# The low halves of every second K and V weight tile by accumulating DMA, and S5 chunks issued one place earlier

## The chip, the cores and the metric

The kernel runs on one core of one Trainium2 chip. The metric is the device time of one execution in microseconds (us). The engines are TensorE (PE, matmuls, with PEld for its weight loads), VectorE (DVE), ScalarE (ACT), GpSimd (POOL) and SyncE (SP, which here only issues DMAs). Everything is float32 in the reference; the kernel reaches that precision by splitting each operand into a high part of type float32r and a low part, which is the remainder.

## The reference

One encoder layer over 256 tokens of width 2048, then a final RMSNorm:

```python
hn = rms_norm(h, norm_mix_g); proj = hn @ w_in           # (256 x 2048) @ (2048 x 3072): conv a, conv gate, ssm u
yc = conformer_conv_group(conv_a, conv_gate, ...)        # a * sigmoid(gate), causal depthwise conv of width 31, layer norm, silu
ys = s5_group(ssm_u, ...)                                # complex diagonal scan over time, 64 groups, then gelu and a 1024 x 1024 GLU
h = h + concat(rms_norm(yc), rms_norm(ys)) @ w_out
hn = rms_norm(h, norm_mem_g); mem_n = rms_norm(mem, mem_norm_g)
h = h + mem_cross_attention(hn, mem_n, w_q, w_kv, w_o)   # kv = mem_n @ w_kv is (256 x 2048) @ (2048 x 4096)
h = h + peer(rms_norm(h), ...)                           # product-key experts, gathered rows of two 16384 x 2048 tables
return rms_norm(h, final_norm_g)
```

The change concerns `mem_n @ w_kv` (its first 2048 columns are K, the others V) and the order in which the parts of `s5_group` are issued.

## The kernel before

A planner orders the instructions of each engine: it takes the program in order, with priorities, and simulates the engines with its own costs; `tc.high_priority(offset=n)` lets what stands inside be ordered as if it had come n instructions earlier. On the chip each engine then runs its own list strictly in that order and waits on semaphores. Tile pools are rings: a tile with `bufs=n` can be written again when all readers of the tile n places before it are done.

`linear` (L147) is the matrix product of all large weights. For each chunk of 512 output columns it walks over eight pairs of 128 rows (index `j`, KG = 2). For each pair it

- loads a weight tile `w_raw` of 128 x 2 x 512 float32 (512 KB) by a DMA from SP (L155, a ring of five);
- on ACT casts it to `w_hi` (L162, a ring of three), on DVE subtracts to get `w_lo` (L163, a ring of three);
- on PE makes three products, activations high by weight high, high by low and low by high (L172 to L174 where the output has tokens on the partitions, as V has; L181 to L183 where it has columns on the partitions, as K and `w_in` have).

All of that but the matmuls is given AHEAD = 500 places of priority. Where a caller gives `whole`, the last pair (`j` = 7) is not split: `whole_matmuls` (L133) multiplies `w_raw` itself in full float32 (L143 for K and `w_in`, L140 for V), and its `w_raw` stays occupied until those matmuls are done. So a chunk of K or V has seven split tiles and one whole one; K and V have four chunks each, 56 split tiles and 8 whole ones.

The order of the program around the change is: the third part of `w_in` (ssm u), the set-up of S5 (tables, BT, CT), then `w_in` in four chunks a0, g0, a1, g1 (each the product of 512 columns; a is the conv input, g its gate), the norm of `mem`, four chunks of K, four of V, the GLU (`zh`, `zl`, weight `ssm_glu_w`), the norm of the S5 half, half of `w_out`, the convolution (L565 and L568: 248 DVE instructions of 128x256, last in the program and so with the lowest priority, but possible from the time that the gates are done), its norm, and the other half of `w_out`.

S5 works in eight chunks q. `s5_next` (L473) issues `s5_tables(q + 1)` (sines and cosines by ACT and DVE) and `s5_body(q)`: 24 small PE matmuls (L445), products and eight scans on DVE (L446 to L462), 32 PE matmuls (L466) and the update of `uT` on DVE (L469). It is issued with 700 places of priority. Before the change it is called after each of a0, g0, a1, g1 and after each K chunk: eight calls for eight chunks.

POOL has no work between its set-up and the end of this part of the kernel; it is used for gathers from 855 us on.

Of the kernel before, what the change touches and what calls it, by code (L numbers as in the profile page):

```python
# [9 lines left out]
F32 = mybir.dt.float32  # L10
F32R = mybir.dt.float32r
# [3 lines left out]
AF = mybir.ActivationFunctionType  # L15
ALU = mybir.AluOpType
# [4 lines left out]
P = 128  # L21
T = 256
NTT = T // P
D = 2048
KT = D // P
# [4 lines left out]
KG = 2  # L30
AHEAD = 500
# [29 lines left out]
W_IN, W_K, W_V = True, True, True  # L61
# [3 lines left out]
SETTLE_RATE = 2.4  # L65
SETTLE_AT = 185
LAG = 2
R_BY = ('AAAA', 'AAVA')


@with_exitstack
def trunk(ctx, tc, a, out, dbg=None):
    nc = tc.nc
    V, S, G, PE, SY = nc.vector, nc.scalar, nc.gpsimd, nc.tensor, nc.sync
# [45 lines left out]
    uctx = ctx.enter_context(ExitStack())  # L120
    with ExitStack() as wctx:
        atx = wctx.enter_context(ExitStack())
        wp = wctx.enter_context(tc.tile_pool(name="wp", bufs=3, side="right"))
        at = atx.enter_context(tc.tile_pool(name="at", bufs=1))
        psm = wctx.enter_context(tc.tile_pool(name="psm", bufs=3, space=PSUM))
        pst = wctx.enter_context(tc.tile_pool(name="pst", bufs=2, space=PSUM))
# [7 lines left out]
        def whole_matmuls(ps, x, raw, j, begin, end, rows_out):  # L134
            for i in range(KG):
                k = (j - (KT // KG - NWHOLE)) * KG + i
                first, last = begin and i == 0, end and i == KG - 1
                if rows_out:
                    for tt in range(NTT):
                        PE.matmul(ps[tt], x[:, k, tt * P:(tt + 1) * P], raw[:, i, :], start=first, stop=last)  # L140
                else:
                    for cb in range(4):
                        PE.matmul(ps[cb // 2][:, cb % 2, :], raw[:, i, cb * P:(cb + 1) * P], x[:, k, :],  # L143
                                  start=first and cb % 2 == 0, stop=last and cb % 2 == 1, skip_group_check=True)

        def linear(x, w, c0, ncol, evac, rows_out, kt=KT, korder=None, ahead=AHEAD, whole=None, cols=None):
            xh, xl = x  # L147
            js = korder or range(kt // KG)
            for n, (c, w_) in enumerate(cols or [(c, 512) for c in range(c0, c0 + ncol, 512)]):
                ncb = w_ // P  # L150
                ps = [psm.tile([P, 512] if rows_out else [P, 2, T], F32, name="mm", tag="mm") for _ in range(2)]
                for m, j in enumerate(js):
                    with tc.high_priority(offset=ahead):
                        raw = wp.tile([P, KG, w_], F32, name="w_raw", bufs=5)
                        SY.dma_start(raw, w[j * KG * P:(j + 1) * KG * P, c:c + w_].rearrange("(k p) c -> p k c", p=P))  # L155
                        full = whole is not None and j >= kt // KG - NWHOLE
                        if full:
                            whole_matmuls(ps, whole, raw, j, m == 0, m == len(js) - 1, rows_out)
                            continue
                        hi = wp.tile([P, KG, w_], F32R, name="w_hi")  # L160
                        lo = wp.tile([P, KG, w_], F32R, name="w_lo")
                        S.copy(hi, raw)  # L162
                        V.tensor_sub(lo, raw, hi.bitcast(F32))  # L163
                    for i in range(KG):
                        k = j * KG + i
                        first, last = m == 0 and i == 0, m == len(js) - 1 and i == KG - 1
                        ah, al = xh[k // 4][:, k % 4, :], xl[k // 4][:, k % 4, :]
                        if rows_out:
                            for tt in range(NTT):
                                o = ps[tt]  # L170
                                ts = slice(tt * P, (tt + 1) * P)
                                PE.matmul(o, ah[:, ts], hi[:, i, :], start=first, stop=False)  # L172
                                PE.matmul(o, ah[:, ts], lo[:, i, :], start=False, stop=False)  # L173
                                PE.matmul(o, al[:, ts], hi[:, i, :], start=False, stop=last)  # L174
                        else:
                            for cb in range(ncb):
                                o = ps[cb // 2][:, cb % 2, :]
                                end = cb % 2 == 1 or cb == ncb - 1
                                wh = hi[:, i, cb * P:(cb + 1) * P]
                                wl = lo[:, i, cb * P:(cb + 1) * P]  # L180
                                PE.matmul(o, wh, ah, start=first and cb % 2 == 0, stop=False, skip_group_check=True)  # L181
                                PE.matmul(o, wh, al, start=False, stop=False, skip_group_check=True)  # L182
                                PE.matmul(o, wl, ah, start=False, stop=last and end, skip_group_check=True)  # L183
                for half in range((ncb + 1) // 2):
                    evac(n, half, ps[half])
                yield n
# [9 lines left out]
        with ExitStack() as mctx:  # L196
# [276 lines left out]
            def s5_next():  # L473
                q = s5["q"]
                if q < CQ:
                  with tc.high_priority(offset=S5_AHEAD):
                    now = s5["tables"]
                    s5["tables"] = s5_tables(q + 1) if q + 1 < CQ else None
                    s5_body(q, now)
                    s5["q"] = q + 1  # L480

            for n in range(2):
                run(linear(xT, a["w_in"], n * 512, 512, ev_a(n), False, whole=xW if W_IN else None))
                s5_next()
                run(linear(xT, a["w_in"], CH + n * 512, 512, ev_g(n), False, whole=xW if W_IN else None))
                s5_next()
            memT, memW = load_mem(a["mem"], a["mem_norm_g"])
# [8 lines left out]
                S.copy(t, ps)  # L496
                SY.dma_start(v_dram[:, tt, 512 * n:512 * n + 512], t)

            for _ in linear(memT, a["w_kv_mem"], 0, D, ev_k, False, whole=memW if W_K else None):
                s5_next()  # L500
            kv_v = linear(memT, a["w_kv_mem"], D, D, ev_v, True, whole=memW if W_V else None)
            run(kv_v)
            for j in range(2):
                z = uT[:, 4 * j:4 * j + 4, :]
# [56 lines left out]
            for k in range(CW):  # L561
                for q in range(CQ):
                    src = cpad[:, q, k:k + T]
# [10 lines left out]
            for q in range(CQ):  # L574
                S.activation(acc[:, q, :], acc[:, q, :], AF.Silu, bias=colv[:, 2, q:q + 1],
                             scale=colv[:, 1, q:q + 1])
# [162 lines left out]
        for n in range((KD + 3) // 4):  # L739
            w = min(KD - 4 * n, 4)  # L740
# [256 lines left out]
    def settle():  # L997
        groups = P // 4
        for tt in range(NTT):
            held = {}  # L1000
            for n in range(groups + LAG):
                if n < groups:
                    held[n] = extract(routes[tt], n)
                    yield
                if n >= LAG:
                    pick(routes[tt], n - LAG, *held[n - LAG])
                    yield
                if tt and n < groups:
                    build(routes[0], n, R_BY[0], "ut", 2)
                    yield  # L1010
# [32 lines left out]
    for g in range(P // 4):  # L1043
        build(routes[1], g, R_BY[1], ("sy", "ut")[g % 2], 2)
    uctx.close()
# [68 lines left out]
    for tt, st in enumerate(sts):  # L1114
        for c, cs_ in enumerate([slice(DC, D)] + COLS):
            src = h3[tt][:, cs_] if c else accg[tt]
# [36 lines left out]
```

## Time and profile before

| | |
|---|---|
| median of 3 runs | 2125.04 us (2120.92 to 2128.39) |
| the profiled execution | 2121.98 us, span 2120.0 us |
| mean granted TensorE clock in it | 0.972 |
| busy shares of the span | PE 93%, DVE 83%, ACT 48%, POOL 35% |
| DMA issues of the weights concerned | `w_raw<-in_w_kv_mem` x64, 512.0 KB each |

In the views of the profile, a row of windows gives the busy time of each engine in a stretch of the span, the granted clock of TensorE as a part of 1, the share of the 16 DMA engines' time in use, and GB/s. A row of waits says who waited for whom, the us in total, how often, and the longest. A row of groups gives the engine, the operation, out<-in, the shape, the count, then busy us and mean ns of one, then the idle time just before. A row of the timeline gives start and length in us, and in brackets the idle time before and what ended it.

### The profile page before, as it was taken

How to read it: one execution, taken by the hardware profiler on the slowest of the kernel's cores; microseconds unless marked ns; L12 is line 12 of the kernel's file. 1: busy time of each engine (PE TensorE's matmuls, PEld its weight loads, DVE VectorE, ACT ScalarE, POOL GpSimd, SP SyncE). 2: the span in 40 equal slices, each digit the busy share in tenths (PEclk: the TensorE clock that was granted, in tenths of full speed). 3: DMA queues.
4: the chain of work that ended last, by engine and by line, in shares of the span. 5: the costliest groups of instructions: out<-in, count | busy, mean ns of one | idle time of the engine just before them, and what ended most of it. 6: DMA issues, size and time to landing. Idle time of an engine off the chain costs nothing.

```text
span 2120.0 us, 32032 instructions
## 1 busy us (share of the span) xinstructions
PE 1970.8 (93%) x11619; PEld 1698.4 (80%) x11619; DVE 1760.7 (83%) x2855; ACT 1024.5 (48%) x1746; POOL 736.2 (35%) x548
## 2 busy tenths in 40 slices
PE   8998798999999999899999999689879999999997
PEld 7987786668799988788888888577667888888886
DVE  5789999987665566999986667998888999899997
ACT  5764544436454454333333333578793444444444
POOL 0000000000000002535446665543218877677772
PEclk9999989999999999999999999899999999999998
DMA  7554454554865476798999999998629999999995
GB/s 246 166 179 154 125 149 130 161 177 139 291 222 193 140 232 221 283 321 319 317 336 402 402 406 391 370 327 275 205 90 318 373 348 337 348 336 340 336 340 187
DMA packets 199390, 563.41 MB, mean 266 GB/s; under 512 B 32050, under 2 KB 40866, under 8 KB 199105
## 3 DMA queue, kind: packets, MB, share of 16 engines
q1 hardware_dynamic: 141888, 318.08, 45.5%
q0 software_dynamic: 57344, 243.30, 30.5%
q8 instruction: 91, 1.49, 0.3%
q14 instruction: 67, 0.54, 0.1%
HBM read 549.38 MB, written 11.93 MB: 265 GB/s over the span
## 4 chain that ended last, share of the span: by engine, by line
PE 48%; DVE 25%; issue 13%; POOL 6%; DMA 5%; ACT 2%; SPq 0%; DVEq 0%; POOLq 0%; ACTq 0%
PE acc L1100 8%; PE acc L1101 8%; PE acc L1099 8%; DVE u L861 6%; POOL u L859 5%; PE mm L183 4%; PE mm L181 4%; PE mm L182 4%; DVE acc L568 3%; DVE w_lo L163 3%; PE mm L174 2%; PE mm L173 2%; PE mm L172 2%; PE y L932 1%; DMA hnT<-ib_dram 1%
## 5 line engine op out<-in xcount | busy, mean ns | idle before, releaser
L861 DVE SCALAR_TENSOR_TENSOR u<-u,hnF 128x1280 f32<-128x1280 f32 x256 | 388.6, 1520 | 86.0 <-DMA u<-in_peer_u,uidx 84.6
L1064 POOL DMA_INDIRECT v<-in_peer_v,vidx x256 | 385.7, 1507 | 178.5 <-DVE accg L1066 68.5
L859 POOL DMA_INDIRECT u<-in_peer_u,uidx x256 | 308.1, 1204 | 328.2 <-DVE u L861 254.0
L162 ACT CAST w_hi<-w_raw 128x1024 fp32r<-128x1024 f32 (+2 forms) x228 | 231.4, 1018 | 289.1 <-PE mm L182 125.7
L901 PE MATMUL sy<-hnT,ut 128*128 128x256 f32 x1536 | 357.0, 385 | 7.9 <-ACT ut L897 7.3
L163 DVE TENSOR_TENSOR w_lo<-w_raw,w_hi 128x1024 fp32r<-128x1024 f32 (+2 forms) x228 | 270.8, 1190 | 111.5 <-ACT w_hi L162 111.3
L901 PEld LDWEIGHTS sy<-hnT,ut 128*128 128x128 f32 x1536 | 287.3, 193 | 48.6 <-ACT ut L897 11.9
L103 ACT CAST vh<-vr 128x1472 fp32r<-128x1472 f32 x128 | 183.2, 1431 | 271.0 <-PE acc L1100 165.8
L1100 PE MATMUL acc<-vh,wl 128*128 128x512 f32 (+1 forms) x768 | 296.7, 386 | 4.4 <-DVE wl L1090 4.3
L183 PE MATMUL mm<-aT_hi,w_lo 128*128 128x256 f32 x960 | 273.2, 293 | 27.2 <-DVE w_lo L163 27.1
L1101 PE MATMUL acc<-vl,wh 128*128 128x512 f32 (+1 forms) x768 | 295.9, 386 | 0.0
L742 POOL TENSOR_TENSOR hnT<-aT_hi,aT_lo 128x1024 f32<-128x1024 f32 (+1 forms) x2 | 3.8, 1908 | 814.5 <-ACT w_hi L162 814.5
L181 PE MATMUL mm<-aT_hi,w_hi 128*128 128x256 f32 x960 | 279.0, 294 | 4.0 <-DVE sg L264 2.3
L1099 PE MATMUL acc<-vh,wh 128*128 128x512 f32 (+1 forms) x768 | 276.5, 385 | 3.2 <-ACT vh L103 2.2
L182 PE MATMUL mm<-aT_lo,w_hi 128*128 128x256 f32 x960 | 276.4, 290 | 0.0
L104 DVE TENSOR_TENSOR vl<-vr,vh 128x1472 fp32r<-128x1472 f32 x128 | 216.5, 1692 | 39.6 <-ACT vh L103 36.9
L1066 DVE SCALAR_TENSOR_TENSOR accg<-v,coef,accg 128x576 f32<-128x576 f32 x256 | 208.7, 815 | 12.0 <-DMA v<-in_peer_v,vidx 7.4
L183 PEld LDWEIGHTS mm<-aT_hi,w_lo 128*128 128x128 f32 x960 | 185.5, 197 | 34.9 <-DVE w_lo L163 31.5
L181 PEld LDWEIGHTS mm<-aT_hi,w_hi 128*128 128x128 f32 x960 | 188.5, 197 | 8.3 <-DVE sg L264 2.9
L182 PEld LDWEIGHTS mm<-aT_lo,w_hi 128*128 128x128 f32 x960 | 189.0, 197 | 1.3 <-issue 0.4
L897 ACT COPY ut<-ut 128x768 f32<-128x768 f32 x128 | 100.4, 801 | 165.8 <-PE ut L895 145.9
L1100 PEld LDWEIGHTS acc<-vh,wl 128*128 128x128 f32 x768 | 145.2, 189 | 35.8 <-DVE wl L1090 5.4
(345 smaller groups left out, 3368.6 us busy)
## 6 DMA issues: line engine op xcount, KB each, us to landing
vr<-in_peer_v SPq DMA_DIRECT2D x128, 736.0 KB
raw<-in_peer_u SPq DMA_DIRECT2D x128, 384.0 KB
w_raw<-in_w_kv_mem SPq DMA_DIRECT2D x64, 512.0 KB
w_raw<-in_w_in SPq DMA_DIRECT2D x48, 512.0 KB
w_raw<-in_w_out SPq DMA_DIRECT2D x32, 512.0 KB
w_raw<-in_w_q_mem SPq DMA_DIRECT2D x32, 512.0 KB
w_raw<-in_w_o_mem SPq DMA_DIRECT2D x32, 512.0 KB
hnT<-ib_dram SPq DMA_DIRECT2D x18, 256.0 KB
```

The source lines that it names most:

```text
L162: S.copy(hi, raw)
L163: V.tensor_sub(lo, raw, hi.bitcast(F32))
L181: PE.matmul(o, wh, ah, start=first and cb % 2 == 0, stop=False, skip_group_check=True)
L182: PE.matmul(o, wh, al, start=False, stop=False, skip_group_check=True)
L183: PE.matmul(o, wl, ah, start=False, stop=last and end, skip_group_check=True)
L859: G.indirect_dma_start(out=u, out_offset=None, in_=a["peer_u"].rearrange("e (q c) -> (e q) c", c=GU), in_offset=bass.IndirectOffsetOnAxis( ...
L861: V.scalar_tensor_tensor(u, u, 1.0, hnF[:, self.tt, :], op0=ALU.mult, op1=ALU.mult, accum_out=self.act[:, j:j + 1])
L901: PE.matmul(ps[:, b % 2, :], ut[:, k, :], hnT[:, k, :], start=k == 0 and b % 2 == 0, stop=k == KD - 1 and b % 2 == 1, skip_group_check=True)
L1064: G.indirect_dma_start(out=v, out_offset=None, in_=table, in_offset=bass.IndirectOffsetOnAxis(ap=vidx[tt][:, j:j + 1], axis=0))
L1099: PE.matmul(o, wh[:, tt, :], vh[:, cs_], start=b == 0, stop=False)
L1100: PE.matmul(o, wl[:, tt, :], vh[:, cs_], start=False, stop=False)
L1101: PE.matmul(o, wh[:, tt, :], vl[:, cs_], start=False, stop=b == NB - 1)
```

## The change

Three things change.

1. In the K and V products, tiles with odd place `m` in their chunk (1, 3 and 5; place 7 is the whole tile) get their low part in another way: ACT writes the negated, rounded tile into `w_lo`, and a DMA issued from POOL adds the weights to it from memory, reading the same 512 KB a second time. The DVE subtraction of these tiles is gone.
2. The rings are resized for every `linear`: `w_raw` five to four, `w_lo` three to four, `w_hi` stays three.
3. `s5_next()` is called once more ahead of a0, so each S5 chunk is issued one call earlier and the last call (after the fourth K chunk) finds nothing left to do.

```diff
+RAW_BUFS = 4
+HI_BUFS = 3
+LO_BUFS = 4
...
-        wp = wctx.enter_context(tc.tile_pool(name="wp", bufs=3, side="right"))
+        wp = wctx.enter_context(tc.tile_pool(name="wp", bufs=HI_BUFS, side="right"))
...
-                        raw = wp.tile([P, KG, w_], F32, name="w_raw", bufs=5)
-                        SY.dma_start(raw, w[j * KG * P:(j + 1) * KG * P, c:c + w_].rearrange("(k p) c -> p k c", p=P))
+                        raw = wp.tile([P, KG, w_], F32, name="w_raw", bufs=RAW_BUFS)
+                        src = w[j * KG * P:(j + 1) * KG * P, c:c + w_].rearrange("(k p) c -> p k c", p=P)
+                        SY.dma_start(raw, src)
...
                         hi = wp.tile([P, KG, w_], F32R, name="w_hi")
-                        lo = wp.tile([P, KG, w_], F32R, name="w_lo")
+                        lo = wp.tile([P, KG, w_], F32R, name="w_lo", bufs=LO_BUFS)
                         S.copy(hi, raw)
-                        V.tensor_sub(lo, raw, hi.bitcast(F32))
+                        if dma_lo and m % 2:
+                            S.activation(lo, raw, AF.Copy, scale=-1.0)
+                            G.dma_start(lo, src, accum_op=ALU.add)
+                        else:
+                            V.tensor_sub(lo, raw, hi.bitcast(F32))
...
+            s5_next()
             for n in range(2):
                 run(linear(xT, a["w_in"], n * 512, 512, ev_a(n), False, whole=xW if W_IN else None))
                 s5_next()
...
-            for _ in linear(memT, a["w_kv_mem"], 0, D, ev_k, False, whole=memW if W_K else None):
+            for _ in linear(memT, a["w_kv_mem"], 0, D, ev_k, False, dma_lo=True, whole=memW if W_K else None):
                 s5_next()
-            kv_v = linear(memT, a["w_kv_mem"], D, D, ev_v, True, whole=memW if W_V else None)
+            kv_v = linear(memT, a["w_kv_mem"], D, D, ev_v, True, dma_lo=True, whole=memW if W_V else None)
```

More of the change, by code (lines that the diff above doesn't have):

```diff
@@ L144, in whole_matmuls, with linear @@
                                   start=first and cb % 2 == 0, stop=last and cb % 2 == 1, skip_group_check=True)
-        def linear(x, w, c0, ncol, evac, rows_out, kt=KT, korder=None, ahead=AHEAD, whole=None, cols=None):
+        def linear(x, w, c0, ncol, evac, rows_out, kt=KT, korder=None, dma_lo=False, ahead=AHEAD, whole=None, cols=None):
             xh, xl = x
```

## The prediction

> **What bounds the kernel now.** I read the windows by stage first, then the waits inside the stage that the change touches, then its groups by shape, then single timelines. The change acts from about 100 us to about 500 us; before and behind that only the ring sizes differ.
>
> ```profile
> 100.00:120.00 20.00, 18.96 (x155) 17.73 (x154) 18.41 (x27) 10.43 (x13) 0.00 (x0) 0.95 0.60 177
> 120.00:140.00 20.00, 20.00 (x159) 16.88 (x159) 12.61 (x18) 11.13 (x25) 0.00 (x0) 0.96 0.58 185
> 160.00:460.00 300.00, 264.07 (x1668) 216.18 (x1667) 300.00 (x486) 132.86 (x179) 0.00 (x0) 0.94 0.49 148
> 460.00:500.00 40.00, 35.66 (x258) 31.51 (x257) 25.70 (x29) 21.06 (x23) 0.00 (x0) 0.96 0.48 154
> 560.00:580.00 20.00, 20.00 (x92) 15.98 (x91) 12.46 (x15) 8.75 (x14) 0.00 (x0) 1.00 0.99 307
> 600.00:700.00 100.00, 100.00 (x841) 100.00 (x840) 59.71 (x85) 49.32 (x70) 0.00 (x0) 1.00 0.53 175
> ```
>
> The columns are the stretch, its length, busy us of PE, PEld, DVE, ACT and POOL, the granted clock, the DMA share and GB/s. From 160 to 460 us DVE is busy for all 300 us: in this stretch DVE sets the pace, and in the others shown it has idle time. PE is second. Its 264.07 us at a clock of 0.94 are 264.07 x 0.94 = 248 us of work at full clock, so 300 us could at best become 248: 36 us are idle and 16 us are lost to the clock. From 600 us on PE is busy without a break.
>
> ```profile
> PE mm L183 <- DVE w_lo L163: 21.4, 9, 5.4
> PE mm L173 <- DVE w_lo L163: 10.3, 3, 5.5
> PE mm L181 <- DVE sg L264: 2.3, 1, 2.3
> ```
>
> ```profile
> ACT w_hi L162 <- PE mm L182: 60.7, 20, 12.0
> ACT w_hi L162 <- PE mm L174: 47.6, 19, 5.3
> ```
>
> These are waits in the same stretch. Of PE's 36 us idle, 21.4 + 10.3 = 31.7 us are waits for `w_lo` from DVE, in 12 stops of up to 5.5 us. ACT waits on PE for a free `w_hi`: it runs ahead as far as the ring of three allows.
>
> ```profile
> L568 DVE SCALAR_TENSOR_TENSOR acc<-cpad,cwT,acc 128x256 f32<-128x256 f32 x231 | 98.1, 474 | 0.0
> ...
> L163 DVE TENSOR_TENSOR w_lo<-w_raw,w_hi 128x1024 fp32r<-128x1024 f32 x65 | 78.7, 1212 | 0.0
> L162 ACT CAST w_hi<-w_raw 128x1024 fp32r<-128x1024 f32 x64 | 66.8, 1046 | 113.5 <-PE mm L182 60.7 <-PE mm L174 47.6 <-DVE acc L565 1.8
> ...
> L425 ACT ACTIVATE cs<-cs 128x1024 f32<-128x1024 f32 x5 | 5.3, 1056 | 0.0
> ```
>
> The largest thing on DVE there is the convolution (98.1 us), which the planner uses to fill; the `w_lo` tiles are next (78.7 us).
>
> **The change part by part.**
>
> *DVE loses* three subtractions in each of eight chunks: 24 x 1.212 us = 29.1 us of the 300. That is also a bound on what this part can bring by DVE. On PE's side, the waits on DVE can give back at most 31.7 us. Four of seven split tiles still go by DVE, so if each kept its wait, 18 us would stay; with 29 us of room in DVE's list I take half of that, 9 us, because the planner will still put convolution instructions ahead of a tile. So this term is 31.7 - 9 = **23 us gained**.
>
> *ACT gains* 24 negating copies of the shape of L425, 24 x 1.056 = 25.3 us. ACT is busy for 132.86 of 300 us and most of its idle time is the wait for a free `w_hi` (113.5 us), so this costs nothing where it stands, but a `w_hi` or an evacuation queued behind one of them comes 1.06 us later, and the copy itself lies on the way of the odd tile. If that cover were gone the cost would be the 25.3 us.
>
> *The odd tile's new way* is what can cost. Where DVE took a subtraction, there is now cast, negation, descriptor work on POOL, and an accumulating transfer. No accumulating transfer is in this trace, so I bound it.
>
> ```profile
> L859 POOL DMA_INDIRECT u<-in_peer_u,uidx x256 | 308.1, 1204 | 328.2 <-DVE u L861 254.0
> ```
>
> ```profile
> 163.47 4.52 DMA xc<-in_mem
> ...
> 562.07 8.37 DMA w_raw<-in_w_out
> 574.85 9.16 DMA w_raw<-in_w_out
> ```
>
> ```profile
> q1 hardware_dynamic: 23018, 44.09, 48.9%
> ```
>
> POOL takes 1.2 us for a gather of 128 rows; this transfer has 256 rows of 2 KB, so I take 1.9 us between 1.2 and 3.0. POOL has nothing else to do then, so nobody queues behind its wait but the next such transfer. The chain of waits has a plain 512 KB load landing after 4.52 us with two other loads just ahead of it, and after 8.37 and 9.16 us where the DMA engines are 0.99 busy. The last row is queue 1 in the stretch 160 to 460: 44.09 MB in 48.9% of 300 us, that is 300 GB/s, or 1.74 us of all 16 engines for 512 KB. Without the two loads ahead I estimate 4.52 less part of 3.5 us, about 3.7 us; the accumulating one has to read `w_lo` too, so I add 1.7 us: 5.4 us, nearest to the lightly loaded row because the share here is 0.49. The 24 transfers bring 24 x 2 x 1.74 = 84 us of engine time into a stretch with 153 us free (0.51 x 300). The way of an odd tile from its free `w_hi` is then 1.05 + 1.06 + 1.9 + 5.4 = 9.4 us; the ends are 1.05 + 1.06 + 1.2 + 4.5 = 7.8 us and 1.05 + 1.06 + 3.0 + 9.2 = 14.3 us.
>
> The Trainium skill, "DMA: Bandwidth & Descriptors", section "Anatomy of one DMA — SWDGE (gpsimd) path", gives for a transfer issued from GpSimd 2.0 us and the bytes over 436 GB/s, an estimate of 3.2 us for 512 KB, and no run here shows it for one that adds. By that the way is about 7.2 us and the sum below comes to about 2094 us. Against it, the Trainium skill, "Collectives: The Full Stack", section "The bandwidth ceiling: the fold count and why AG ≠ RS ≠ AR", says that an adding transfer is slower because the add needs two source reads; this trace has no such transfer.
>
> What has PE to do meanwhile?
>
> ```profile
> 440.51 1.06 ACT L162 CAST w_hi<-w_raw 128x1024 fp32r<-128x1024 f32 x1 [3.20 <-PE mm L174]
> 443.32 1.05 ACT L162 CAST w_hi<-w_raw 128x1024 fp32r<-128x1024 f32 x1 [1.75 <-PE mm L174]
> ```
>
> ```profile
> 235.28 1.89 PE L143 MATMUL mm<-x_whole,w_raw 128*128 128x256 f32 x8
> 237.10 0.39 PE L445 MATMUL bu<-uh,BT 32*128 32x256 f32 x2
> ```
>
> ```profile
> 235.38 0.34 SPq L492 DMA_DIRECT2D k_dram<-kv_ev  x1
> 237.20 0.37 SPq L155 DMA_DIRECT2D w_raw<-in_w_kv_mem  x1
> ```
>
> At its own pace PE uses a split tile in 443.32 - 440.51 = 2.81 us and a whole one in about 3.6 us (two groups like the one at 235.28). `w_hi` is a ring of three, so an odd tile starts on its way when the tile three places before it is done, with two tiles, 5.6 us, of PE work left. Between chunks the whole tile adds its 3.6 us, 9.2 in all. At 9.4 us the first odd tile of a chunk is 0.2 us late. For the second there is something else: the whole tile holds its `w_raw` until PE is through. The rows show this: its last matmuls end at about 237.1 us, and SP issues the next load at 237.20. With five buffers that load is tile 4 of the next chunk, an even one. With four it is tile 3, an odd one: it lands 3.7 us later and then needs 9.4 us, 13.1 in all, against three tiles of PE work, 8.4 us: **4.7 us late, an added wait**. Its lateness covers the third odd tile. So 4.9 us a chunk, 8 x 4.9 = 39 us. S5's matmuls can lie in these gaps: 24 of L445 (12 of them from 237.10 to 238.0, so 1.8 us) and 32 of L466.
>
> ```profile
> 224.61 0.64 PE L466 MATMUL yp<-t,CT 128*32 128x256 f32 x8
> 225.18 0.38 PE L181 MATMUL mm<-aT_hi,w_hi 128*128 128x256 f32 x1
> ```
>
> Eight of L466 hold PE for 0.57 us, so 32 are 2.3 us, with L445 4.1 us in each S5 chunk. With about six S5 chunks in the stretch this is 25 us of cover if they all fall well; I take 20. **New waits: 39 - 20 = 19 us lost.** PE is behind a waiting matmul with all that follows in its list, the S5 matmuls and thereby DVE's scans too.
>
> *S5 one place earlier.* Its work stays the same, its place moves.
>
> ```profile
> 99.57 0.68 DVE L446 TENSOR_TENSOR zr<-bu,cs 128x512 f32<-128x512 f32 x1
> ...
> 468.21 0.48 DVE L469 SCALAR_TENSOR_TENSOR uT<-uT,colv,yp 128x256 f32<-128x256 f32 x1
> ...
> 477.37 1.23 DVE L163 TENSOR_TENSOR w_lo<-w_raw,w_hi 128x1024 fp32r<-128x1024 f32 x1 [5.25 <-ACT w_hi L162]
> ```
>
> ```profile
> 458.56 0.68 PE L183 MATMUL mm<-zh,w_lo 128*128 128x256 f32 x1
> ...
> 470.92 0.50 PE L181 MATMUL mm<-zh,w_hi 128*128 128x256 f32 x2 [1.14 <-ACT zh L103]
> ```
>
> Chunk 0 cannot come much before its present 99.57 us, since it needs the set-up; the later ones come up to one `w_in` chunk earlier, into 100 to 140 us, where DVE has 40 - 31.0 = 9.0 us idle. That moves 9 us of DVE work out of the full stretch at best and costs PE in 100 to 140 us what it then waits for late `w_lo` of `w_in`; PE is 38.96 of 40 busy there. I count 2 us gained, between -5 and 9. At the other end S5 ends at 468.2 us, 10 us behind the first GLU matmul, whose second half must wait for it; from 460 to 500 us PE has 4.3 us idle and 0.04 x 35.7 = 1.4 us lost to the clock. With S5 done before V this is mostly gone: **4 us gained**. No DMA moves with S5; POOL's list is empty there, and SP's list holds no load of S5's.
>
> *The rings for the other products.* `w_raw` of four means one load less ahead. From 600 to 700 us PE has no gap at a DMA share of 0.53, and a load of 4 to 5 us against 11 us of ring costs nothing. Only about 550 to 590 us, with the share at 0.99, is there a chain through loads (8.37 and 9.16 us); there the bandwidth is the limit, not the depth. I take 0, at worst 4 us.
>
> **The sum** against the profiled execution: 2121.98 - 23 + 19 - 2 - 4 = 2112 us. The clock: 36 us idle become about 36 - 23 + 19 = 32, so about 16 x 4 / 36 = 2 us less lost: **2110 us**. That execution lies 3 us under the median of the runs, which is 2125.04, so against the median it is 15 us less. About 0.3%, 6 us, is what a measurement of this kernel tells from no change.
>
> **The rivals.**
>
> *The transfer is hidden anyway.* Then PE waits for neither DVE nor DMA: 31.7 us gained, 4 + 2 from S5, and half of the clock's 16 us with the stops gone: 2122 - 31.7 - 6 - 8 = 2076, or about 2084 with 8 us of new waits left. For it speaks the DMA share of 0.49 and that the planner can put S5 matmuls in front of an odd tile. Against it the way of 7.8 us at least, over the 5.6 us of cover.
>
> *The transfer is slow and PE stops on odd tiles (slower).* With the row of 8.37 us for the transfer the way is 1.05 + 1.06 + 1.5 + 8.4 = 12.0 us: first odd tile 12.0 - 9.2 = 2.8 late, second 3.7 + 12.0 - 8.4 - 2.8 = 4.5, third 12.0 - 5.6 - 4.5 = 1.9, 9.2 us a chunk, 74 us, less 25 us of S5 cover: 49 us against 29 gained, so 2122 + 20 = 2142 us. It decides from new waits of 29 us on, (29 + 20) / 8 = 6.1 us a chunk, a way of about 10.1 us: not far from the 9.4 that I take. For it speaks that an adding transfer reads twice and that raw loads run beside it.
>
> *The room on DVE is filled at once (no change).* The planner fills DVE's list by its own costs with convolution; if an even tile then waits as long as before (18 us stay, not 9) and S5's end isn't reached earlier, the sum is 2122 - 14 + 19 - 2 - 2 = 2123 us. For it speaks that DVE shows no idle time in 300 us though the convolution isn't urgent.
>
> **How the numbers follow.** The forecast of 2110 has 0.42, the hidden transfer 0.20, the slow one 0.25, no change 0.13. Faster by over 0.3%: 0.39 of the forecast's and all of the hidden one's, 0.59. Within 0.3%: 0.03 of the forecast's and 0.12 of the third rival's, 0.15. Slower: 0.25 and 0.01, 0.26. The range 2086 to 2140 leaves out about half of the hidden case and half of the slow one. Since cases of both signs are in it, the likeliest one's own range is 2098 to 2118.
>
> **What would show it.** In the changed profile: `w_lo` on DVE 24 fewer; a queue from POOL with 24 transfers of 512 KB between 180 and 450 us; ACT 25 us more. If I am right, DVE has idle time before 460 us, waits of PE on `w_lo` from DVE are below 12 us, and PE waits on the DMA of `w_lo` for 10 to 25 us, mostly at the second odd tile of a chunk. The last L469 comes before the last V matmul. The end of V comes before 450 us. Wrong would be: PE waits on that DMA of over 30 us (slow rival) or of next to nothing (hidden); DVE without a gap until the same 460 us (third); or a loss from 600 us on, which would be the rings.

## The result, and the profile after

The changed kernel takes 2113.52 us (median of 7 runs, 2109.43 to 2116.8) beside 2128.39 us for the kernel before on the same chip (7 runs, 2120.92 to 2133.78): a ratio of 0.993, interval 0.9913 to 0.9947. That is 14.9 us less. The profiled execution took 2113.52 us, with a span of 2111.8 us and a mean granted clock of 0.973. In the changed kernel the cast is L166, the negation L168, the transfer L169, the subtraction L171; K's and `w_in`'s products are L189 to L191, V's L180 to L182; S5's update of `uT` is L477, the convolution L577.

The windows of the changed kernel, with the columns used before:

```profile
160.00:430.00 270.00, 252.91 (x1639) 206.93 (x1639) 263.54 (x448) 153.38 (x202) 29.19 (x24) 0.97 0.78 211
430.00:460.00 30.00, 21.43 (x144) 16.37 (x145) 20.74 (x27) 7.76 (x9) 0.00 (x0) 0.72 0.35 104
```

The full stretch now ends at 430 us instead of 460, and DVE has 6.5 us idle in it. But a hole has opened behind it: from 430 to 460 us PE is idle for 8.6 us and the granted clock is 0.72. The landmarks are in the rows of three tiles (durations min/median/max in ns, then first and last start in us). Before:

```profile
L469 DVE SCALAR_TENSOR_TENSOR uT<-uT,colv,yp x8: 466/472/481, 139.1 to 468.2; 128x256 f32<-128x256 f32 x8
L496 ACT COPY kv_ev<-mm x8: 587/588/589, 372.1 to 459.2; 128x512 f32<-128x512 f32 x8
L183 PE MATMUL mm<-zh,w_lo x64: 276/276/682, 458.6 to 489.0; 128*128 128x256 f32 x64
L597 DVE TENSOR_TENSOR h<-h,mm x16: 677/680/689, 562.3 to 810.9; 128x512 f32<-128x512 f32 x16
```

After:

```profile
L477 DVE SCALAR_TENSOR_TENSOR uT<-uT,colv,yp x8: 465/476/479, 139.5 to 449.9; 128x256 f32<-128x256 f32 x8
L505 ACT COPY kv_ev<-mm x8: 565/587/588, 346.0 to 431.9; 128x512 f32<-128x512 f32 x8
L191 PE MATMUL mm<-zh,w_lo x64: 276/276/580, 431.8 to 470.9; 128*128 128x256 f32 x64
L606 DVE TENSOR_TENSOR h<-h,mm x16: 679/681/689, 545.4 to 796.3; 128x512 f32<-128x512 f32 x16
```

V ends 27.3 us earlier (459.2 to 431.9). S5 ends only 18.3 us earlier, so that it now comes 18.0 us behind V instead of 9.0. The GLU, which needs it, ends 18.1 us earlier, and the last `h` 14.6 us. So 9 of the 27 us were given back at S5's end, and 3.5 us between there and 800 us.

The waits of PE, then of ACT, from 140 to 500 us (total us, times, longest). The first two rows are of the kernel before, the others of the changed one:

```profile
PE mm L183 <- DVE w_lo L163: 23.6, 12, 5.4
PE mm L173 <- DVE w_lo L163: 10.3, 3, 5.5
```

```profile
PE mm L191 <- DVE w_lo L171: 9.3, 5, 4.5
PE mm L191 <- DMA w_lo<-in_w_kv_mem: 6.7, 6, 2.0
PE mm L181 <- DMA w_lo<-in_w_kv_mem: 4.6, 5, 2.2
```

```profile
ACT w_lo L168 <- DMA w_raw<-in_w_kv_mem: 18.3, 12, 6.1
ACT w_hi L166 <- DMA w_raw<-in_w_kv_mem: 14.5, 7, 4.0
ACT uT L514 <- DVE uT L477: 10.9, 1, 10.9
```

23.6 + 10.3 = 33.9 us of waits on DVE became 9.3 us (from 160 to 460 us, 31.7 became 8.7), and 6.7 + 4.6 = 11.3 us of waits on the transfers were added. The third row of ACT is the hole: the Gelu of S5's result waits 10.9 us for the last `uT`. The first two are loads that come late for ACT, by 32.8 us in all. The kernel before has no such wait from 160 to 460 us, and the ring sizes alone bring 21.9 us of them (8 times, in the run with the rings alone below); without the adding transfers the changed kernel has 7.5 us. So the ring of four and the transfers both have a part in it.

The groups by shape and the DMA queues from 160 to 460 us:

```profile
L171 DVE TENSOR_TENSOR w_lo<-w_raw,w_hi 128x1024 fp32r<-128x1024 f32 x45 | 54.7, 1217 | 10.0 <-ACT w_hi L166 9.9
L169 POOL DMA_DIRECT2D w_lo<-in_w_kv_mem x24 | 29.2, 1216 | 381.5 <-ACT w_lo L168 313.7 <-DVE acc L577 30.1 <-ACT uh L106 16.4
L168 ACT ACTIVATE w_lo<-w_raw 128x1024 fp32r<-128x1024 f32 x24 | 25.4, 1059 | 18.3 <-DMA w_raw<-in_w_kv_mem 18.3
```

```profile
q1 hardware_dynamic: 24632, 47.18, 47.4%
q0 software_dynamic: 6528, 12.58, 25.5%
```

A transfer costs POOL 1.216 us; in the kernel before, POOL has nothing to do from its set-up until 816 us, and its first gather starts at 839 us (not 855). On the DMA engines the 24 take 25.5% of 300 us, 76.5 us, or 3.19 us of all 16 engines each, against 47.4% of 300 us for 47.18 MB, 1.58 us per 512 KB, for plain loads: twice as much for the same bytes. That they go through POOL's queue, q0, doesn't explain it: the plain gathers of the changed kernel go through q0 too, and from 900 to 1000 us they take 58.7 us of all 16 engines for 21.09 MB, or 1.46 us for 512 KB (in packets of 4.5 KB instead of 1.9 KB):

```profile
q0 software_dynamic: 4642, 21.09, 58.7%
```

The Trainium skill, "Collectives: The Full Stack", section "The bandwidth ceiling: the fold count and why AG ≠ RS ≠ AR", says of the adding step of a ReduceScatter that it is slower because the add needs two source reads. The factor 2.0 here fits that; no run here separates the second read from the add.

### The profile page after: what moved, and what is told of

Read it like the earlier page. It is cut to its first block, busy times and chain, and to the rows that moved or that the text cites. A ratio compares the mean times of both kernels' runs of the same rounds, so it can differ in the third digit from the quotient of the medians.

```text
span 2111.8 us, 32091 instructions
## 1 busy us (share of the span) xinstructions
PE 1969.9 (93%) x11619; PEld 1695.0 (80%) x11619; DVE 1731.7 (82%) x2831; ACT 1047.3 (50%) x1770; POOL 776.1 (37%) x572
## 4 chain that ended last, share of the span: by engine, by line
PE 43%; DVE 21%; issue 14%; DMA 12%; POOL 6%; ACT 4%; SPq 0%; DVEq 0%; POOLq 0%; ACTq 0%
PE acc L1109 7%; PE acc L1110 7%; PE acc L1108 7%; DVE u L870 6%; POOL u L868 5%; PE mm L191 3%; PE mm L190 3%; PE mm L189 3%; DMA w_lo<-in_w_kv_mem 3%; PE mm L181 3%; PE mm L182 3%; PE mm L180 3%; DVE acc L577 2%; DMA v<-in_peer_v,vidx 2%; DVE w_lo L171 1%
## 5 line engine op out<-in xcount | busy, mean ns | idle before, releaser
L1073 POOL DMA_INDIRECT v<-in_peer_v,vidx x256 | 396.2, 1548 | 171.8 <-PE pw L975 61.6
L166 ACT CAST w_hi<-w_raw 128x1024 fp32r<-128x1024 f32 (+2 forms) x228 | 231.4, 1017 | 255.9 <-PE mm L182 93.9
L171 DVE TENSOR_TENSOR w_lo<-w_raw,w_hi 128x1024 fp32r<-128x1024 f32 (+2 forms) x204 | 239.8, 1179 | 114.4 <-ACT w_hi L166 114.2
L191 PE MATMUL mm<-aT_hi,w_lo 128*128 128x256 f32 x960 | 273.2, 292 | 17.1 <-DVE w_lo L171 10.1
L189 PE MATMUL mm<-aT_hi,w_hi 128*128 128x256 f32 x960 | 277.0, 291 | 2.6 <-ACT w_hi L166 2.6
L191 PEld LDWEIGHTS mm<-aT_hi,w_lo 128*128 128x128 f32 x960 | 183.4, 194 | 24.7 <-DVE w_lo L171 13.6
L189 PEld LDWEIGHTS mm<-aT_hi,w_hi 128*128 128x128 f32 x960 | 186.5, 195 | 6.3 <-ACT w_hi L166 3.5
L169 POOL DMA_DIRECT2D w_lo<-in_w_kv_mem x24 | 29.2, 1216 | 381.5 <-ACT w_lo L168 313.7
```

The costliest lines, as they stand in the source:

```text
L1073: G.indirect_dma_start(out=v, out_offset=None, in_=table, in_offset=bass.IndirectOffsetOnAxis(ap=vidx[tt][:, j:j + 1], axis=0))
```

## The experiments

The question was which part of the change brings the 15 us, and why the new waits stayed at 11 us. Ratios are to the kernel before in the same comparison (its medians were 2124.8 to 2125.6 us), with their interval; two versions from different comparisons are set against each other by these ratios, of which 0.001 is 2.1 us.

**One part alone.** First the changed kernel without the earlier S5 chunk, so that only the transfers and rings remain:

```diff
-            s5_next()
```

> The changed kernel without the extra S5 call: low halves by accumulating DMA and the resized rings alone. Theory A (VectorE's list sets the length of the K and V stage, so the 24 subtractions taken off it are the gain): the last V evacuation stays near 430 to 436 us, as in the changed kernel (431.9), and the time is 10 to 18 us under the kernel before, a ratio of 0.9915 to 0.9955. Theory B (the S5 move carries a good part of it, at the end of the stage): the last uT update comes 8 to 15 us later than in the changed kernel (449.9), the last GLU matmul at 478 us or later instead of 470.9, and the time is at most 8 us under the kernel before.

Measured 2113.24 us, 0.9939 (0.9924 to 0.9953), with the end of V at 434.1 us: the first theory. Then the kernel before with only that call added:

```diff
+            s5_next()
```

> The kernel before with the extra S5 call alone, old rings, all low halves on VectorE. Theory A: VectorE stays without idle time from 160 to 460 us, the uT updates of S5 shift by less than 5 us, the time is within 5 us of the kernel before (ratio 0.9977 to 1.0023). Theory B: S5 ends before the last V matmul, the last GLU matmul comes 6 to 12 us before 489.0, ratio 0.993 to 0.997.

Measured 2123.24 us, 0.9989 (0.9978 to 1.0): the first theory. The last `uT` came 2.4 us earlier than before (465.8 us), and so did the first, by 2.3 us (136.8 us). The traces say more: the added call moves no instruction. On DVE, ACT, POOL and SP the instructions, by their tiles, stand in the same order up to 800 us with the call and without it, in this pair as in the changed kernel and the version without the call; on PE all but 0.3% of the records agree. On DVE, 0, 21, 47, 97, 140, 190, 225 and 240 convolution instructions (L568) stand ahead of the eight `uT` updates both times. So 2 us is about what this comparison shows between two kernels of one order.

And the ring sizes alone, as the changed kernel without the added call and without the transfers:

```diff
-            s5_next()
...
-            for _ in linear(memT, a["w_kv_mem"], 0, D, ev_k, False, dma_lo=True, whole=memW if W_K else None):
+            for _ in linear(memT, a["w_kv_mem"], 0, D, ev_k, False, dma_lo=False, whole=memW if W_K else None):
...
-            kv_v = linear(memT, a["w_kv_mem"], D, D, ev_v, True, dma_lo=True, whole=memW if W_V else None)
+            kv_v = linear(memT, a["w_kv_mem"], D, D, ev_v, True, dma_lo=False, whole=memW if W_V else None)
```

> The kernel before with the resized rings alone (raw four, low halves four), all low halves on VectorE, S5 in its old place. If the shallower load ring costs something in the w_out stage (in the changed kernel ScalarE waits 12.5 us for loads of w_out between 480 and 600 us, before 4.4 us): 2 to 5 us slower, ratio 1.001 to 1.0025, with those waits near 12 us. If it costs nothing: within 2 us, waits near 4.4 us.

Measured 2126.65 us, 1.0012 (1.0001 to 1.0024). So the transfers, with their ring, bring what can be measured; the added call does nothing, and the rings alone cost some 2.5 us (2126.65 beside 2124.82 us by the medians, 0.0012 by the ratio, little more than that 2 us). Their price shows in ACT's waits for the loads of `w_out` from 480 to 600 us (497 to 617 us before). Before, after and with the rings alone:

```profile
ACT w_hi L162 <- DMA w_raw<-in_w_out: 4.4, 2, 3.3
```

```profile
ACT w_hi L166 <- DMA w_raw<-in_w_out: 12.5, 6, 6.3
```

```profile
ACT w_hi L166 <- DMA w_raw<-in_w_out: 11.2, 7, 5.4
```

**The ring of loads.** The prediction put the late odd tiles down to the load ring of four. With five, the `w_lo` ring has to go back to three to fit the memory:

```diff
-RAW_BUFS = 4
+RAW_BUFS = 5
-LO_BUFS = 4
+LO_BUFS = 3
```

> The changed kernel with the rings of the kernel before (raw five, low halves three). Theory of the prediction (the whole tile holds one of four load buffers, so the second odd tile of a chunk is loaded late): ScalarE's waits for loads before negating (18.3 us, 12 times) fall below 6 us, TensorE's waits for the accumulating DMA (11.3 us) below 6 us, the w_out stage gets back 2 to 4 us; in all 3 to 8 us under the changed kernel, ratio to the kernel before 0.989 to 0.992. Rival (the ring of low halves is what an odd tile needs, as its buffer is taken for longer): the waits for the accumulating DMA rise above 15 us and the time is the changed kernel's or up to 6 us more.

Measured 2126.05 us, 1.0008 (0.9993 to 1.0022): the whole gain is gone. The waits of PE:

```profile
PE mm L191 <- DMA w_lo<-in_w_kv_mem: 21.2, 8, 4.8
PE mm L181 <- DMA w_lo<-in_w_kv_mem: 13.9, 9, 3.8
```

35.1 us of waits on the transfers instead of 11.3. ACT's waits for the loads of `w_kv_mem` are gone from 160 to 460 us, as the prediction's theory had it, but PE's waits on the transfers rose, as the rival had it. Which of the two sizes does it? The changed kernel with the `w_lo` ring alone at three:

```diff
-LO_BUFS = 4
+LO_BUFS = 3
```

> The changed kernel with three buffers for low halves instead of four; load ring four as changed. Theory A (the fourth buffer of low halves lets ScalarE write the negated tile one tile before its own cast, and that is the lead that hides the transfer): TensorE's waits for the accumulating DMA rise from 11.3 us to 25 to 40 us, as with raw five and low halves three (35.1 us), and the time is 8 to 15 us over the changed kernel, ratio to the kernel before 0.997 to 1.003. Theory B (it was the load ring of five against four that undid the gain there): waits stay near 11 us and the time near the changed kernel's, ratio 0.992 to 0.995.

Measured 2127.68 us, 1.0009 (0.9995 to 1.0022), with waits of PE of

```profile
PE mm L191 <- DMA w_lo<-in_w_kv_mem: 21.9, 8, 5.0
PE mm L181 <- DMA w_lo<-in_w_kv_mem: 16.2, 9, 4.5
```

It is the ring of `w_lo`; the load ring of five changes 38.1 to 35.1 us.

**The lead of the negation.** The prediction's chain was cast, negation, transfer. But the negation reads `w_raw` alone and needs only a free `w_lo`. ACT's timeline of the changed kernel:

```profile
213.91 1.05 ACT L168 ACTIVATE w_lo<-w_raw 128x1024 fp32r<-128x1024 f32 x1
...
216.76 1.03 ACT L166 CAST w_hi<-w_raw 128x1024 fp32r<-128x1024 f32 x1
```

Counting casts and negations along ACT's list, 23 of the 24 negations stand ahead of the cast of their own tile; here the negation has a lead of 2.9 us on it. With the `w_lo` ring of three it is 10 of 24, and none of K's twelve. To take the lead away and keep the ring, the negation was made from the cast tile:

```diff
-    S.activation(lo, raw, AF.Copy, scale=-1.0)
+    S.activation(lo, hi.bitcast(F32), AF.Copy, scale=-1.0)
```

> The changed kernel with the negated tile read from the tile's own cast instead of from the raw load: the same values, the same sizes, the same four buffers, but the negation now has to come after the cast, as the prediction assumed. Theory A (the lead of one tile, which the fourth buffer allows, hides the transfer): TensorE's waits for the accumulating DMA rise from 11.3 us to 25 us or more and the time is 8 to 15 us over the changed kernel, ratio to the kernel before 0.997 to 1.003, as with three buffers (1.0009). Rival (the fourth buffer helps in another way, such as a freer order on ScalarE): waits below 18 us, ratio 0.992 to 0.996.

Measured 2134.83 us, 1.0041 (1.0028 to 1.0054): slower than the kernel before. ACT's timeline (each negation now follows its cast, 24 of 24), then PE's waits:

```profile
239.28 1.05 ACT L166 CAST w_hi<-w_raw 128x1024 fp32r<-128x1024 f32 x1 [2.30 <-PE mm L190]
240.36 1.06 ACT L168 ACTIVATE w_lo<-w_hi 128x1024 fp32r<-128x1024 f32 x1
```

```profile
PE mm L191 <- DMA w_lo<-in_w_kv_mem: 19.4, 8, 3.8
PE mm L181 <- DMA w_lo<-in_w_kv_mem: 14.4, 4, 4.2
```

33.8 us, as the first theory had it, and a time 21 us over the changed kernel, more than either theory gave. So both are needed: a slot of `w_lo` that is free early, and a copy that doesn't stand behind the cast, which waits for a free `w_hi`. This is the slow rival of the prediction, brought about by one operand.

**What the transfers cost.** The transfer taken out, with the negation left:

```diff
-    G.dma_start(lo, src, accum_op=ALU.add)
```

> The changed kernel without the accumulating transfers: the odd tiles of K and V keep the negated high part as their low part, the weights are not added to it. All else is the same. Theory A (VectorE's list still sets the pace of the K and V stage, the transfers are nearly covered): the last V evacuation comes at most 5 us before 431.9 us, the time is 0 to 4 us under the changed kernel, ratio to the kernel before 0.991 to 0.993. Theory B (the transfers and the loads that they push aside are what is left): TensorE's 11.3 us of waits for them and ScalarE's 32.8 us of waits for loads go, the last V evacuation comes 10 us or more earlier, and the time is 8 us or more under the changed kernel, ratio at most 0.989.

Measured 2106.2 us, 0.9919 (0.9904 to 0.9933). The median is 7 us below the changed kernel's, between the two expectations; by the ratios it is 2 us, with intervals that overlap. In the traces V ends 7.6 us earlier (424.3 instead of 431.9). So the transfers and the late loads cost between 2 and 8 us, less than PE's 11.3 us of waits on the transfers. One reason shows: without the transfers PE waits longer for DVE, 17.0 us instead of 9.3, most of it in this row:

```profile
PE mm L190 <- DVE w_lo L170: 15.3, 11, 4.5
```

More tiles by transfer (places 0, 2, 4, 6 of a chunk, 32 in all):

```diff
-    if dma_lo and m % 2:
+    if dma_lo and m % 2 == 0:
```

> The changed kernel with the tiles of even place (0, 2, 4, 6) taking the accumulating DMA instead of those of odd place: 32 transfers instead of 24, eight subtractions, 9.7 us, less on VectorE. If VectorE's list still sets the pace: the last V evacuation comes 5 to 10 us before 431.9, the time is 0 to 8 us under the changed kernel, ratio 0.9895 to 0.993. If the transfers and the loads beside them are what is left (the run without them was 7 us faster): TensorE's waits for the DMA rise from 11.3 to 20 us or more, ratio 0.993 to 0.998.

Measured 2118.78 us, 0.9983 (0.9966 to 1.0001): most of the gain is gone, with 26.9 us of waits on the transfers, as the second theory had it. Both the number of transfers and their places differ from the changed kernel here, and no run tells the two apart:

```profile
PE mm L181 <- DMA w_lo<-in_w_kv_mem: 14.6, 5, 6.1
PE mm L191 <- DMA w_lo<-in_w_kv_mem: 12.3, 6, 5.1
```

**S5's end.** Does a higher priority bring S5 in front of the convolution?

```diff
-S5_AHEAD = 700
+S5_AHEAD = 1400
```

> The changed kernel with 1400 instead of 700 places of priority for S5. In the changed kernel the last uT update (449.9 us) comes 18 us after the last V evacuation (431.9), and the GLU waits for it at a low granted clock. Theory A (S5's place in VectorE's list is what holds the end): the last uT update comes before 440 us, the last GLU matmul 6 to 14 us before 470.9, the time is 4 to 12 us under the changed kernel, ratio to the kernel before 0.987 to 0.991. Rival (S5 pushed ahead delays the w_in and K tiles by as much): the last V evacuation comes as much later, ratio 0.992 to 0.995.

Measured 2110.21 us, 0.9939 (0.9924 to 0.9953), the changed kernel's time within the intervals. The last `uT` stays where it was (449.3 us), and so does V's end (431.3 us). The reason is that this edit, too, moves nothing: DVE's and ACT's instructions stand in the order of the changed kernel, with 0, 21, 50, 98, 150, 204, 232 and 240 convolution instructions ahead of the eight `uT` updates both times. Priority doesn't reach it, and the run can't say what an earlier S5 would bring. The convolution was then made shorter in the kernel before:

```diff
-    for k in range(CW):
+    for k in range(CW - 9):
```

> The kernel before with 22 of the 31 taps of the convolution: 72 VectorE instructions of about 0.395 us each, 28 us, are left out of the computation, and nothing else. Theory A (the length of the K and V stage is VectorE's list, so any 28 us taken off it come back one to one): the last V evacuation moves from 459.2 us to 430 to 436 us and the time falls by 10 to 28 us, ratio 0.987 to 0.9955. Theory B (it is the waits for the low halves that count, not the list): TensorE's waits for low halves from VectorE stay near 32 us, the last V evacuation moves by less than 12 us, ratio 0.996 or more.

Measured 2108.29 us, 0.9921 (0.9908 to 0.9934), with no transfer at all. Its tiles:

```profile
L469 DVE SCALAR_TENSOR_TENSOR uT<-uT,colv,yp x8: 475/493/550, 139.0 to 435.3; 128x256 f32<-128x256 f32 x8
L496 ACT COPY kv_ev<-mm x8: 574/588/590, 363.9 to 446.9; 128x512 f32<-128x512 f32 x8
L568 DVE SCALAR_TENSOR_TENSOR acc<-cpad,cwT,acc x168: 472/516/556, 149.2 to 382.4; 128x256 f32<-128x256 f32 x168
```

V ends 12 us earlier than before, but S5 ends 33 us earlier: the convolution is over at 382 us, and S5's last chunks find DVE free. That points to the order of DVE's list as what held S5. The time is in the range of the first theory, but its mechanism holds only in part: 28 us taken off the list moved V's end by 12 us and not by 28, and 27.4 us of PE's 33.9 us of waits on DVE's `w_lo` stayed (140 to 500 us). A shorter list alone doesn't bring `w_lo` in time; why these waits stay was not tried. For an earlier end of S5 the convolution need not be left out; part of it can be put later. In the changed kernel the start of its last two channel blocks (31 taps each, 62 of 248 instructions; the expectations say 64) was made to depend on S5's seventh chunk, by a bias `late` that is `colv` plus zero times a value of that chunk:

```diff
+            late = mp.tile([P, CQ], F32, name="late")
+            V.scalar_tensor_tensor(late, bc(uT[:, 6, 0:1], [P, CQ]), 0.0, colv[:, 0, :], op0=ALU.mult, op1=ALU.add)
...
-                        V.tensor_scalar(acc[:, q, :], src, cwT[:, q, 0:1], colv[:, 0, q:q + 1], op0=ALU.mult,
+                        V.tensor_scalar(acc[:, q, :], src, cwT[:, q, 0:1], (late if q >= 6 else colv[:, 0, :])[:, q:q + 1], op0=ALU.mult,
```

> The changed kernel with the convolution of the last two of eight channel blocks held back: its bias is read through a copy that depends on S5 chunk 6, so 64 of the 248 convolution instructions, about 25 us of VectorE time, cannot run before about 424 us. Theory A (the convolution, put early into VectorE's full list, is what makes S5 end at 449.9 us, 18 us after V, and the GLU wait): the last uT update comes at 435 us or earlier, the last GLU matmul 8 to 18 us before 470.9, the time 6 to 15 us under the changed kernel, ratio to the kernel before 0.986 to 0.990. Rival (S5's end hangs on its own chain, not on the convolution): the last uT update stays within 5 us of 449.9 and the time is the changed kernel's or up to 10 us more, because the held-back part now ends later.

Measured 2102.22 us, 0.9886 (0.9861 to 0.9911), the fastest version here: about 9 us below the changed kernel (0.993 - 0.9886 = 0.0044), and the first theory. A window and two tiles:

```profile
430.00:460.00 30.00, 28.63 (x224) 26.69 (x223) 29.19 (x56) 17.87 (x19) 0.00 (x0) 1.00 0.58 186
```

```profile
L477 DVE SCALAR_TENSOR_TENSOR uT<-uT,colv,yp x8: 466/480/483, 137.9 to 431.0; 128x256 f32<-128x256 f32 x8
L505 ACT COPY kv_ev<-mm x8: 567/588/591, 343.7 to 429.3; 128x512 f32<-128x512 f32 x8
L191 PE MATMUL mm<-zh,w_lo x64: 276/280/682, 428.7 to 454.4; 128*128 128x256 f32 x64
```

The hole is filled: PE 28.63 of 30 us busy at a clock of 1.00, S5's end 1.7 us behind V's. Last, the same edit in the kernel before, with no transfer:

```diff
+            late = mp.tile([P, CQ], F32, name="late")
+            V.scalar_tensor_tensor(late, bc(uT[:, 6, 0:1], [P, CQ]), 0.0, colv[:, 0, :], op0=ALU.mult, op1=ALU.add)
...
-                        V.tensor_scalar(acc[:, q, :], src, cwT[:, q, 0:1], colv[:, 0, q:q + 1], op0=ALU.mult,
+                        V.tensor_scalar(acc[:, q, :], src, cwT[:, q, 0:1], (late if q >= 6 else colv[:, 0, :])[:, q:q + 1], op0=ALU.mult,
```

> The kernel before, without accumulating transfers, with the convolution of the last two of eight channel blocks held back until the seventh S5 chunk is done (64 of 248 convolution instructions, some 25 us of DVE's list). Theory A: what bounded 160 to 460 us was the length of DVE's list, and anything not urgent that leaves it counts, by whichever way: as where 72 convolution instructions were left out, V ends some 12 us earlier, S5 ends before 445 us, and the ratio is about 0.992 to 0.995, that is about as much as the whole change brings. Theory B: the late tiles of w_lo wait for ACT and the planner's order and not for the list's length, and the held-back work is only paid later, between 440 and 510 us: the ratio is 0.998 to 1.002, and the gain of the held-back convolution in the changed kernel hung on the room that the transfers had made.

Measured 2115.66 us, 0.9954 (0.994 to 0.9967), 9.9 us less: nearer to the first theory, just above its range of ratios. Its tiles:

```profile
L469 DVE SCALAR_TENSOR_TENSOR uT<-uT,colv,yp x8: 473/541/597, 138.3 to 442.1; 128x256 f32<-128x256 f32 x8
L496 ACT COPY kv_ev<-mm x8: 561/583/589, 361.3 to 449.5; 128x512 f32<-128x512 f32 x8
L183 PE MATMUL mm<-zh,w_lo x64: 277/280/679, 448.8 to 471.6; 128*128 128x256 f32 x64
```

S5 now ends before V, V ends 9.7 us earlier and the GLU 17.4 us earlier. Holding back the convolution brings about 10 us without the transfers and about 9 us with them: the two gains nearly add up.

## Why the prediction was right, and where it was not

The time, 2110 us, was 3.5 us off, and the fall of 12 us against its profiled execution (15 against the median) is near the 14.9 us measured. But several terms were off and cancelled: the new waits and the loss to the clock were 8 and 6 us smaller than forecast, and S5's end and the later stages took most of that back. That the sum came so near is luck in part.

- *Waits on DVE, 23 us gained:* right. From 160 to 460 us 31.7 us became 8.7, where 9 were forecast.
- *New waits on the transfer, 19 us lost:* 11.3 us, and the way was mis-built. POOL's part is 1.2 us, not 1.9. The transfer itself was about as long as forecast or longer. Two rows, of POOL and of PE:

```profile
215.25 1.20 POOL L169 DMA_DIRECT2D w_lo<-in_w_kv_mem  x1 [8.98 <-ACT w_lo L168]
```

```profile
221.42 0.38 PE L191 MATMUL mm<-aT_hi,w_lo 128*128 128x256 f32 x1 [1.66 <-DMA w_lo<-in_w_kv_mem]
```

  From POOL's start to PE's release are 6.2 us here, and 6.2 to 10.7 us in the eleven transfers that PE waited for, with a median of 8.1; 1.9 + 5.4 = 7.3 us had been taken. The step that failed is the start: "the way of an odd tile from its free `w_hi`" has the negation behind the cast, and it runs ahead of it. With the negation bound to the cast, the forecast's chain cost 33.8 us of waits and 2134.83 us: not the 19 us of the sum, but nearly the 39 us that it had before the cover by S5's matmuls was taken off. So the chain as forecast would have given the slow rival, and that the term came out near is luck. The 2.0 us and the bytes over 436 GB/s of the Trainium skill, "DMA: Bandwidth & Descriptors", section "Anatomy of one DMA — SWDGE (gpsimd) path", an estimate of 3.2 us, are a third to a half of the 6.2 to 10.7 us measured at a DMA share of 0.78.
- *The second odd tile late by the load ring of four, 4.7 us a chunk:* there, but much smaller. Of the 18.3 us that the negations wait for their loads, 16.3 us are at the second odd tile, in seven of the eight chunks. Five of PE's eleven stops, with 5.6 of the 11.3 us, are there too, and each of the five is shorter than the load wait of its negation. One of them, on ACT and on PE:

```profile
321.00 1.06 ACT L168 ACTIVATE w_lo<-w_raw 128x1024 fp32r<-128x1024 f32 x1 [2.88 <-DMA w_raw<-in_w_kv_mem]
```

```profile
330.80 0.50 PE L181 MATMUL mm<-w_lo,aT_hi 128*128 128x512 f32 x1 [2.25 <-DMA w_lo<-in_w_kv_mem]
```

  By these rows it cost 0.2 to 2.3 us in five chunks and nothing in three. With the negation bound to the cast the second odd tile has 23.4 of the 33.8 us, though ACT waits only 1.5 us for loads there, so something else adds to it in that run; what it is stays open. The load ring of five doesn't test this alone, because it came with a `w_lo` ring of three, which cost all of the gain by itself.
- *The clock, 2 us less lost:* its input was wrong. From 160 to 430 us PE is idle for 270 - 252.9 = 17 us, not 32, and 252.9 x (1 - 0.97) = 8 us are lost to the clock instead of 16. By the forecast's own proportion, 16 x 17 / 36 is 8. The runs don't show that proportion to be a rule: with the `w_lo` ring of three PE is idle for 43 us from 160 to 460 us at a clock of 0.96, where the kernel before has 36 us at 0.94. So the stretch became 36 - 17 = 19 us shorter by idle time and 8 by the clock: the 27 us at V's end.
- *S5, 2 + 4 us gained:* wrong, the largest miss. "With S5 done before V this is mostly gone" took it that a chunk issued one place ahead would end earlier. But the added call moved no instruction, and with the transfers DVE's list was filled with more convolution (204 instead of 190 instructions ahead of the sixth `uT`, 240 ahead of the last as before): the third rival's mechanism, in one place. V's end moved and S5's did not follow, which gave 9 us back, with ACT waiting 10.9 us and the clock at 0.72. That it was the convolution's place, the held-back version shows.
- *The rings, 0 and at worst 4 us lost:* some 2.5 us alone, with longer waits for the loads of `w_out`.
- *Profiled execution and median:* the trace shows 14.6 us up to the last `h` at 796.3 us, and 8.2 us in the span, so 6 us are lost later. No one stretch stands out. The expert stage's first and last matmuls, before and after:

```profile
L901 PE MATMUL sy<-hnT,ut x1536: 379/379/654, 882.9 to 1324.1; 128*128 128x256 f32 x192
```

```profile
L910 PE MATMUL sy<-hnT,ut x1536: 379/379/636, 871.2 to 1315.6; 128*128 128x256 f32 x192
```

  The first one is 11.7 us earlier and the last one 8.5. The cause was not looked for; the 7 runs of the changed kernel lie within 7.4 us of each other. The median fell by 14.9 us, as much as the first 800 us show.

Of the listed signs, DVE's idle time before 460 us, PE's waits on it below 12 us, 10 to 25 us of waits on the transfers, 24 transfers on POOL, 25 us more of copies on ACT, and V's end before 450 us came true. That the waits are mostly at the second odd tile came half true, and S5's end before V's did not.

## What to carry to other kernels

Where work is moved from a full engine to a transfer, look at what its first step truly depends on and at the ring that it writes: here one more buffer of the result, and a copy that needn't wait for the cast, made the difference between 15 us gained and 2 to 9 us lost. Relief of an engine that a planner fills with work that isn't urgent is filled again; look at what stands next at the end of the stretch, and hold that work back by a dependence if priority doesn't move it. Before crediting an edit that is meant to change an order, compare the orders: two edits here moved nothing. Before adding traffic, ask whether the full list could simply be shortened: the held-back convolution brought two thirds of the gain with no transfer at all.

## What the runs showed of the hardware

An adding transfer took twice the time of a plain load of the same bytes on the DMA engines (3.19 against 1.58 us of all 16 for 512 KB).

The length that a trace records for a DVE instruction is not the pace of the engine. From 340 to 400 us a convolution instruction has a mean of 474 ns in the kernel before, and of 571 ns with the convolution held back in it (544 to 550 ns in the profiles with the shorter convolution and with the higher priority, 530 ns without the adding transfers). But a run of six, with the instruction behind it, looks like this, before, and with the convolution held back:

```profile
366.25 2.45 DVE L568 SCALAR_TENSOR_TENSOR acc<-cpad,cwT,acc 128x256 f32<-128x256 f32 x6
368.63 1.21 DVE L163 TENSOR_TENSOR w_lo<-w_raw,w_hi 128x1024 fp32r<-128x1024 f32 x1
```

```profile
351.68 2.55 DVE L570 SCALAR_TENSOR_TENSOR acc<-cpad,cwT,acc 128x256 f32<-128x256 f32 x6
354.05 1.31 DVE L459 TENSOR_TENSOR t<-zr,cs 128x1024 f32<-128x1024 f32 x1
```

The next instruction starts 2.38 us behind the start of the six in one trace and 2.37 us in the other, so the pace is the same, 0.40 us for one instruction. Only the recorded end comes 0.1 us later, for a short instruction as for a long one (1.31 instead of 1.21 us). These profiles are hardly late by it: with the higher priority, where the order is that of the changed kernel, V and S5 end within 0.6 us of it. Why the ends are recorded later stays open.
